# A hybrid encoder layer: when the next block's input is loaded and normed, and when a head's bias rows are requested

## The chip, the cores and the metric

The kernel is one launch on 1 core of one Trainium2 chip. The metric is the device time of the launch in microseconds, as the median of several runs. The engines are TensorE (PE, with its weight loads as PEld), VectorE (DVE), ScalarE (ACT), GpSimd (POOL) and SyncE (SP), which here only issues transfers. Each runs its own instructions in order and waits for the others by semaphores.

## The reference

One layer over 2048 positions of 1024 features in float32. A norm feeds one projection, whose columns go to a state-space part (512 features) and to attention in chunks (8 heads of 64). Both are normed, concatenated, projected and added to x, and a gated feed-forward part of width 2816 follows.

```python
h = rmsnorm(x, norm_mix_g[l])
proj = h @ w_in[l]                      # u_ssm, q, k, v: 512 columns each
y_ssm = s5_mixer(u_ssm, ...)            # diagonal complex scan over the sequence, GLU
y_att = chunked_attention(q, k, v, attn_rel_bias[l])
mixed = concatenate([rmsnorm(y_ssm, ...), rmsnorm(y_att, ...)])
x = x + mixed @ w_out[l]
h2 = rmsnorm(x, norm_ffn_g[l])
x = x + (silu(h2 @ w_gate[l]) * (h2 @ w_up[l])) @ w_down[l]
return rmsnorm(x, norm_final_g)

# chunked_attention: chunks of 64, each sees itself and 8 before it
bias = rel_bias[:, clip(rel, -128, 128) + 128]
scores = einsum('bnqhd,bnkhd->bhnqk', qc, kb) / sqrt(64) + bias
probs = softmax(where(valid, scores, -1e30))
out = einsum('bhnqk,bnkhd->bnqhd', probs, vb)
```

## The kernel before

All of it is one program. After a prologue (norm and the projection for the state-space part) comes the attention part, roughly 135 to 720 us, in which the scan of the state-space part also runs; then the output projection, the gate and up products, and the down product. Only the attention part is touched by the change.

Numbers of full precision are carried through PE as two parts: a high part `hi`, rounded (L741, on ACT), and the rest `lo` (L742, on DVE). A product takes three matmuls: hi with hi, hi with lo, lo with hi. The line of nearly all matmuls is L76, of transposes L79; `split` (L153) does the same for weights, on ACT and DVE.

The attention part runs 128 steps. The sequence is cut in 4 blocks (`sb`) of 512 positions; a block has 4 pairs of heads (`pr`), a pair two heads (`hh`), a head 4 query tiles (`qp`) of 128. So a block is 32 steps and a head 4. Step 0 of block `sb` is step 32 x sb of the part. In each step:

- `scores`: 2 or 4 matmuls `sc` (one PSUM buffer), then on DVE one instruction (L862) that adds the bias rows `nb`, takes the row extreme into `mn` and frees `sc`, and on ACT the exponential (L865).
- `transp`, two steps later: the tile `s` is transposed into `pt` (one PSUM buffer), which ACT copies as `pth` (L880) and DVE as `ptl` (L881).
- `pv_head` after a head's last tile, `pv_scale` after a pair's: matmuls into `pj`, an addition into `ya` on DVE (L905), a scaling, and a store.

The bias rows of a head lie in HBM (`nbs`) and come into one of two buffers, `nba` for even heads and `nbb` for odd ones, by two transfers on SP (L549, L550). `load_nb` asks for those of the next head while a head is in work.

Between the steps lie units of other work, Python generators that are driven forward in a window of steps: `Unit(gen, n, s0, s1, pre)` starts `pre` steps before `s0` and is spread over s0 to s1. `hT_unit` prepares the next block's input: it loads the transposed x in eight pieces of 128 features (L722), multiplies each with the gain and the norm `rsn` in place (L740) and makes `hi` and `lo`. Pieces 0 to 2 (`DB` = 3) go through one unit and tiles `xt` (a ring of 2); pieces 3 to 7 through another, piece 3 in an `xt`, 4 to 7 in pairs in two tiles `raw`, which in block 0 also hold weights that are to be split. `qk_unit` and `v_unit` make q, k and v of a pair of heads for the block from `hi`, `lo` and weights `w` (L707, 1 MB each): k's low part is L788, its store into `ks` L790, the load of the former block's keys L756. `ssm_front` and `ssm_back` are the scan: loads of `U` (L559), `Tm` (L637) and `Vm`, matmuls `pj<-U,Bst`, a long chain on POOL (L603, L604), and `y` (L651).

The order in which the program is written is not the order in which it stands on each engine: PE keeps the written one, and a scheduler orders DVE, ACT, POOL and SP by it and by what it takes each instruction to cost. SP has one queue: a transfer whose source or whose buffer is not ready holds up all behind it.

Of the kernel before, what the change touches and what calls it, by code (L numbers as in the profile page):

```python
# [13 lines left out]
ALU = mybir.AluOpType  # L14
# [4 lines left out]
KT = D // P  # L19
# [6 lines left out]
H, HD = 8, 64  # L26
SB = 512
NSB = SEQ // SB
# [9 lines left out]
SGB = 2  # L38
RA1, RA2 = 2, 12
QS = 4, 5, 6, 7, 0, 1, 2, 3  # L40
HTA = -12, -9
HTS = -8, -6
HTP = 2
PRO = 0, 0, 2, 2, 2, 2, 0, 0, 0
LIGHT = 0.8
SL = 1
# [2 lines left out]
DB, XB = 3, 2  # L49
# [44 lines left out]
def f32(ap):  # L94
    return ap.bitcast(F32)
# [587 lines left out]
def att_phase(k, ident, S, aw, x0, roots):  # L683

    tc, nc, io, pfs = k.tc, k.nc, k.io, k.pfs
    with ExitStack() as cx:
# [28 lines left out]
        def hT_unit(sb, q0=0, q1=KT):  # L715
            hi, lo = hT.setdefault(sb, ([], []))
            ts = slice(sb * SB, (sb + 1) * SB)
            xts = {}

            def load(q, n=1):  # L720
                t = k.t(aw, "raw", [P, 1024], bufs=2) if n > 1 else k.t(aw, "xt", [P, SB], bufs=XB)
                nc.sync.dma_start(t[:].rearrange("p (q t) -> p q t", q=n), io["xt"][q * P : (q + n) * P, ts].rearrange("(q p) t -> p q t", p=P))  # L722
                for m in range(n):
                    xts[q + m] = t[:, m * SB : (m + 1) * SB]

            if q0 == 0:
                load(0)
                load(1)
            else:
                load(q0)  # L730
                for q in range(q0 + 1, q1, 2):
                    load(q, 2)
            for q in range(q0, q1):
                yield
                if q0 == 0 and q + 2 < q1:
                    load(q + 2)
                xt = xts[q]
                for v, n in zip(hT[sb], ("hi", "lo")):
                    v.append(k.t(aw, f"{n}{q}x" if q < DB and sb % 2 else f"{n}{q}", [P, SB], F32R)[:])
                nc.vector.scalar_tensor_tensor(xt, xt, k.gm[:, q : q + 1], S["rsn"][:, ts], op0=ALU.mult, op1=ALU.mult)  # L740
                nc.scalar.copy(hi[q], xt)  # L741
                nc.vector.tensor_tensor(lo[q], xt, f32(hi[q]), op=ALU.subtract)  # L742
            yield

        def qk_unit(sb, pr):
# [47 lines left out]
        QK_N = 1 + 2 * KT  # L793
# [39 lines left out]
        def load_nb(h):  # L833
            return bias_rows(k, S, h, nbt[h % 2])

        def scores(st):
            sb, pr, hh, qp = st
            h = 2 * pr + hh
            if qp == 0:
                hd = st_head[sb, h] = Head()  # L840
                hd.nb = nbs.pop(h) if nbs else load_nb(h)
                hd.s = {}
                hd.p = None
            hd = st_head[sb, h]
            if qp == 2 and (sb, h) < (NSB - 1, H - 1):
                nbs[(h + 1) % H] = load_nb((h + 1) % H)
            q2h, q2l, k2 = qk[sb, pr][hh]
            k0 = max(qp, 4) if sb == 0 else qp
            nk = (qp + 5 - k0) * P
            half = nk // 2 if nk > 512 else nk  # L850
            nch = nk // half
            ps = k.t(psum2, "sc", [P, 2, 512])
            for c in range(nch):
                c0 = k0 * P + c * half + k2.shape[1] - 2 * SB
                cols = slice(c0, c0 + half)
                for n, q2 in ((0, q2h), (1, q2l)):
                    k.ta.matmul(ps[:, c, :half], q2[:, qp * P : (qp + 1) * P], k2[:, cols], start=n == 0, stop=n == 1)
            s = k.t(aa, "s", [P, 640], bufs=3)
            mn = k.t(aa, "mn", [P, 1], bufs=4)
            if (hh, qp) == (0, 0):  # L860
                sums[sb, pr] = k.t(aa, "sm", [P, 2, 4], bufs=3)
            nc.vector.tensor_tensor_reduce(  # L862
                s[:, :nk].rearrange("p (a b) -> p a b", a=nch), ps[:, :nch, :half],
                hd.nb[:, nk - 1 :: -1].rearrange("p (a b) -> p a b", a=nch), 1.0, 3e38, ALU.add, ALU.min, mn[:])
            nc.scalar.activation(s[:, :nk], s[:, :nk], AF.Exp, bias=mn[:], scale=-1.0, accum_out=sums[sb, pr][:, hh, qp : qp + 1])  # L865
            hd.s[qp] = s, k0
# [69 lines left out]
        sp = tc.alloc_tile_pool(name="ssm", reuse_waits="tile", bufs=1)  # L936
        psum = cx.enter_context(tc.tile_pool(name="aps", bufs=1, space=bass.MemoryType.PSUM, reuse_waits="tile"))
        psum2 = cx.enter_context(tc.tile_pool(name="aps2", bufs=1, space=bass.MemoryType.PSUM, reuse_waits="tile"))
        units = []
        for sb in range(NSB):  # L940
            g0 = sb * 32
            C = CUT if sb < NSB - 1 else CUTL
            if sb > 0:
                if DB:
                    units.append(Unit(hT_unit(sb, 0, DB), 2 + DB, g0 + HTA[0], g0 + HTA[1], 2))
                units += [Unit(hT_unit(sb, DB), 2 + KT - DB, g0 + HTS[0], g0 + HTS[1], HTP), Unit(qk_unit(sb, 0), QK_N, g0 + C[0], g0 + C[1], 3, light=LIGHT)]
            units.append(Unit(v_unit(sb, 0), V_N, g0 + C[1], g0 + C[2], 2, light=LIGHT) if sb else Unit(v0, V_N, *V0, done=1))
            for gen, n, c in ((qk_unit(sb, 1), QK_N, 2), (qk_unit(sb, 2), QK_N, 3), (v_unit(sb, 1), V_N, 4), (qk_unit(sb, 3), QK_N, 5)):
                units.append(Unit(gen, n, g0 + C[c], g0 + C[c + 1], 2, light=LIGHT) if sb else Unit(gen, n + 1, C[c], C[c + 1], 4, light=LIGHT, mid=2))
# [5 lines left out]
        for s in range(N + LAG + 2):  # L955
            if s == OPEN:
                aw.release()
                mix = mix_phase(k, S, lambda: k.t(pfs, "pf", [P, 512]))
                units += [Unit(islice(mix, MIX_N), MIX_N, GSTART, N + LAG, GSTART - OPEN)]
            if s == GSTART:  # L960
                sp.release()
            for o in ORDER:
                if o == "s" and s < N:
                    scores(steps[s])
                elif o == "t" and LAG <= s < N + LAG:
                    transp(steps[s - LAG])
                elif o == "p" and LAG + 1 <= s < N + LAG + 1 and steps[s - LAG - 1][3] == 3:
                    pv_head(steps[s - LAG - 1])
                elif o == "p" and s >= LAG + 2 and steps[s - LAG - 2][2:] == (1, 3):
                    pv_scale(steps[s - LAG - 2])  # L970
                elif o == "f":
                    for u in units:
                        u.advance(s)
# [754 lines left out]
```

## Time and profile before

| | |
|---|---|
| median of 3 runs | 2274.19 us (2266.21 to 2277.7) |
| profiled execution, its own time | 2277.4 us |
| span of that execution | 2275.6 us, so 1.8 us lie outside it |
| mean granted clock of PE | 0.978 |
| PE busy | 2169.8 us, 95% of the span |
| DVE / ACT / POOL busy | 68% / 44% / 15% |

The profile is of one execution, which was 3.2 us slower than the median. In a timeline row stand the start, the duration, engine, line, operation, output<-inputs, shape and count; in brackets the idle time of the engine just before it and what ended that. "SPq" rows are transfers being issued, not their landing.

### The profile page before, as it was taken

What the parts mean: (1) busy time and instruction counts of PE and PEld (TensorE: products, weight loads), DVE (VectorE), ACT (ScalarE), POOL (GpSimd) and SP (SyncE); (2) the same over time, 40 slices, a digit from 0 to 9 for tenths busy, and PEclk for the clock granted to TensorE, in tenths of its full rate; (3) what the DMA queues carried; (4) which work ended last, traced back from release to release, by engine and by line L of the source; (5) the groups of instructions that cost most, each with busy time, mean ns of one, the idle gap of its engine ahead of it and who ended that gap; (6) DMA issues with size and microseconds to landing.
All of it is one profiled execution on the core that took longest, in us unless ns stands there. A gap on an engine that the chain in (4) does not pass through costs nothing.

```text
span 2275.6 us, 30307 instructions
## 1 busy us (share of the span) xinstructions
PE 2169.8 (95%) x10632; PEld 1828.5 (80%) x10632; DVE 1542.7 (68%) x2695; ACT 1002.5 (44%) x1656; POOL 350.1 (15%) x827
## 2 busy tenths in 40 slices
PE   8989898999997899999999999999999999999997
PEld 6778787888986688878888887888888777888886
DVE  7757556555556756776767678666666477688776
ACT  6446555455557452343333335333333443353322
POOL 2246666646520000000000000000000010000000
PEclk9999999999998899999999999999999999999999
DMA  8778875766653535854555467655433395465652
GB/s 296 234 250 263 220 195 172 220 197 185 177 166 105 172 118 160 270 179 144 178 183 193 163 213 259 196 175 185 143 93 115 110 389 169 166 226 182 218 179 75
DMA packets 214874, 428.36 MB, mean 188 GB/s; under 512 B 38848, under 2 KB 61424, under 8 KB 207616
## 3 DMA queue, kind: packets, MB, share of 16 engines
q1 hardware_dynamic: 207072, 401.49, 54.6%
q0 software_dynamic: 7648, 24.92, 3.3%
q8 instruction: 84, 1.38, 0.2%
q14 instruction: 70, 0.57, 0.1%
HBM read 286.86 MB, written 129.00 MB: 183 GB/s over the span
## 4 chain that ended last, share of the span: by engine, by line
PE 77%; DMA 5%; DVE 5%; issue 4%; POOL 3%; ACT 2%; SPq 1%; DVEq 0%; ACTq 0%; POOLq 0%
PE X L76 20%; PE ps L76 17%; PE Y L76 10%; PE big L76 9%; PE pf L76 8%; PE W L76 5%; PE pj L76 3%; PE sc L76 2%; DMA acc<-x 2%; PE pt L79 2%; POOL X L595 1%; POOL X L594 1%; DMA lo<-hc 1%; POOL X L604 1%; POOL fx L603 1%
## 5 line engine op out<-in xcount | busy, mean ns | idle before, releaser
L76 PE MATMUL X<-hi,c 128*128 128x512 f32 x1408 | 451.3, 391 | 6.2 <-DVE c L153 5.5
L76 PE MATMUL ps<-hd,hd 128*128 128x512 f32 (+1 forms) x1968 | 429.7, 380 | 3.9 <-DVE hd L153 2.0
L76 PEld LDWEIGHTS ps<-hd,hd 128*128 128x128 f32 x1968 | 357.6, 189 | 74.6 <-DVE hd L153 2.7
L76 PEld LDWEIGHTS X<-hi,c 128*128 128x128 f32 x1408 | 265.4, 189 | 62.7 <-DVE c L153 6.4
L76 PE MATMUL X<-lo,c 128*128 128x512 f32 x704 | 274.9, 390 | 0.0
L153 ACT CAST hd<-hd 128x1536 fp32r<-128x1536 f32 (+1 forms) x106 | 147.3, 1393 | 234.6 <-DMA hd<-hq 148.1
L76 PE MATMUL Y<-hi,c 128*128 128x512 f32 x704 | 224.7, 390 | 2.1 <-DVE u L1407 2.1
L153 DVE TENSOR_TENSOR hd<-hd 128x1536 fp32r<-128x1536 f32 (+1 forms) x106 | 174.0, 1643 | 37.1 <-ACT hd L153 36.5
L153 DVE TENSOR_TENSOR c<-S,c 128x512 fp32r<-128x512 f32 x176 | 120.8, 687 | 98.9 <-ACT c L153 98.7
L1511 POOL DMA_DIRECT2D hd<-hq x7 | 5.3, 762 | 1169.5 <-PE X L76 1158.0
L1403 ACT COPY u<-X 128x512 f32<-128x512 f32 x132 | 77.3, 586 | 200.6 <-PE X L76 200.6
L76 PE MATMUL big<-m,woh 128*128 128x512 f32 x512 | 163.1, 400 | 0.0
L153 ACT CAST c<-S 128x512 fp32r<-128x512 f32 x176 | 109.3, 621 | 119.0 <-PE Y L76 61.8
L1545 DVE TENSOR_TENSOR acc<-acc,ps 128x512 f32<-128x512 f32 x196 | 130.3, 681 | 41.0 <-PE ps L76 40.7
L76 PEld LDWEIGHTS Y<-hi,c 128*128 128x128 f32 x704 | 132.3, 188 | 30.4 <-DVE u L1407 2.9
L76 PEld LDWEIGHTS X<-lo,c 128*128 128x128 f32 x704 | 132.8, 189 | 27.7
L76 PE MATMUL pf<-hi,w 128*128 128x512 f32 x416 | 150.7, 414 | 0.8 <-ACT hi L741 0.8
L153 ACT CAST c<-raw 128x512 fp32r<-128x512 f32 x132 | 82.2, 622 | 151.0 <-PE Y L76 64.3
L881 DVE TENSOR_TENSOR ptl<-pt,pth 128x640 fp32r<-128x640 f32 (+3 forms) x152 | 98.2, 646 | 66.6 <-ACT pth L880 64.8
L76 PE MATMUL Y<-lo,c 128*128 128x512 f32 x352 | 137.0, 389 | 0.0
L865 ACT ACTIVATE s<-s,mn 128x640 f32<-128x640 f32 (+4 forms) x128 | 97.9, 765 | 74.1 <-DVE mn L862 67.1
L880 ACT CAST pth<-pt 128x640 fp32r<-128x640 f32 (+3 forms) x152 | 83.6, 550 | 82.6 <-PE pt L79 77.6
(448 smaller groups left out, 4280.6 us busy)
## 6 DMA issues: line engine op xcount, KB each, us to landing
w<-wss SPq DMA_DIRECT2D x36, 1024.0 KB, 6.6
hq<-g SPq DMA_DIRECT2D x140, 256.0 KB, 2.1
hd<-hq SPq DMA_DIRECT2D x35, 768.0 KB, 4.5
hd<-wc SPq DMA_DIRECT2D x35, 768.0 KB, 5.9
raw<-in_w_gate SPq DMA_DIRECT2D x44, 512.0 KB, 3.7
raw<-in_w_up SPq DMA_DIRECT2D x44, 512.0 KB, 4.2
wc<-px SPq DMA_DIRECT2D x66, 256.0 KB, 2.9
wss<-w SPq DMA_DIRECT2D x12, 1024.0 KB, 5.8
```

The lines of the kernel that those rows point to most:

```text
L76: return self.tc.keep_in_program_order(self.tc.nc.tensor.matmul(*a, **b))
L79: return self.tc.keep_in_program_order(self.tc.nc.tensor.transpose(*a, **b))
L153: return nc.scalar.copy(hi, raw), nc.vector.tensor_tensor(lo, raw, f32(hi), op=ALU.subtract)
L594: eng.tensor_tensor(dst, dst, t[:, :, :, :n], op=ALU.add)
L595: eng.tensor_tensor(dst, dst, t2[:, :, :, :n], op=ALU.add)
L603: eng.tensor_tensor(t, end[:, e].unsqueeze(3).to_broadcast([P, GP, n, 7]), pw, op=ALU.mult)
L604: eng.tensor_tensor(dst[:, c], dst[:, c], t, op=ALU.subtract if e == 1 and c == 0 else ALU.add)
L865: nc.scalar.activation(s[:, :nk], s[:, :nk], AF.Exp, bias=mn[:], scale=-1.0, accum_out=sums[sb, pr][:, hh, qp : qp + 1])
L880: nc.scalar.copy(pth[:, a:b, qp, :], pt[:, a:b, :])
L881: nc.vector.tensor_tensor(ptl[:, a:b, qp, :], pt[:, a:b, :], f32(pth[:, a:b, qp, :]), op=ALU.subtract)
L1403: nc.scalar.copy(u[:], ps[:])
L1545: V.tensor_tensor(a, a, ps[:], op=ALU.add)
```

## The change

Three things are changed; all matmuls, their number and their order on PE stay as they are.

The window of the unit of pieces 0 to 2 goes from steps -12 to -9 (before the block's first step) to -16 to -13. The unit of pieces 3 to 7 is cut in two: the loads and the norms, one norm for each advance, in steps -13 to -8 with one step ahead, and the hi and lo parts in -8 to -6. The bias rows of the next head are requested in a head's second step (`qp == 1`) instead of its third.

```diff
-HTA = -12, -9
+HTA = -16, -13
 HTS = -8, -6
-HTP = 2
+HTN = -13, -8
...
+            def norm(q):
+                nc.vector.scalar_tensor_tensor(xts[q], xts[q], k.gm[:, q : q + 1], S["rsn"][:, ts], op0=ALU.mult, op1=ALU.mult)
+
             if q0 == 0:
                 load(0)
                 load(1)
...
                 for q in range(q0 + 1, q1, 2):
                     load(q, 2)
+                for q in range(q0, q1):
+                    yield
+                    norm(q)
             for q in range(q0, q1):
                 yield
-                if q0 == 0 and q + 2 < q1:
-                    load(q + 2)
-                xt = xts[q]
+                if q0 == 0:
+                    if q + 2 < q1:
+                        load(q + 2)
+                    norm(q)
...
-                nc.vector.scalar_tensor_tensor(xt, xt, k.gm[:, q : q + 1], S["rsn"][:, ts], op0=ALU.mult, op1=ALU.mult)
-                nc.scalar.copy(hi[q], xt)
-                nc.vector.tensor_tensor(lo[q], xt, f32(hi[q]), op=ALU.subtract)
+                nc.scalar.copy(hi[q], xts[q])
+                nc.vector.tensor_tensor(lo[q], xts[q], f32(hi[q]), op=ALU.subtract)
...
-            if qp == 2 and (sb, h) < (NSB - 1, H - 1):
+            if qp == 1 and (sb, h) < (NSB - 1, H - 1):
                 nbs[(h + 1) % H] = load_nb((h + 1) % H)
...
+        hts = {sb: hT_unit(sb, DB) for sb in range(1, NSB)}
...
-                units += [Unit(hT_unit(sb, DB), 2 + KT - DB, g0 + HTS[0], g0 + HTS[1], HTP), ...]
+                units += [Unit(islice(hts[sb], 1 + KT - DB), 1 + KT - DB, g0 + HTN[0], g0 + HTN[1], 1), Unit(hts[sb], 1 + KT - DB, g0 + HTS[0], g0 + HTS[1]), ...]
```

Behind line 721 the changed file's lines are 5 or 6 higher: the norm is L727, hi L747, lo L748, k's low part L794, L862 is L868 and L881 is L887.

On the engines this gives, at three places, the following order. On DVE at steps 17 to 19, where block 1's input is prepared (`w<-raw` is a weight's split, `lo0x` to `lo2x` are low parts, `nba` marks the bias addition of a step), before:

```order
366 L153 TENSOR_TENSOR w_2436<-raw_2360,w_2436 128x1024
367 L862 ISA s_2402,mn_2403<-sc_2399,nba_106 128x256
369 L881 TENSOR_TENSOR ptl_2293<-pt_2406,pth_2292 128x128
370 L820 SCALAR_TENSOR_TENSOR v_483_2249<-pf_2380,no_1236,v_483_2249 128x4x64
371 L881 TENSOR_TENSOR ptl_2293<-pt_2406,pth_2292 128x3x128
372 L862 ISA s_2447,mn_2448<-sc_2444,nba_106 128x384
374 L740 SCALAR_TENSOR_TENSOR xt_2487<-xt_2487,g_mix_86,rsn_92 128x512
375 L153 TENSOR_TENSOR w_2439<-raw_2362,w_2439 128x1024
376 L742 TENSOR_TENSOR lo0x_2559<-xt_2487,hi0x_2558 128x512
377 L905 TENSOR_TENSOR ya_2279<-pj_2455,yt_2464 64x512
```

and after, from the reduction of step 17 on:

```order
369 L868 ISA s_2420,mn_2421<-sc_2417,nba_106 128x256
371 L887 TENSOR_TENSOR ptl_2293<-pt_2424,pth_2292 128x128
372 L153 TENSOR_TENSOR w_2454<-raw_2364,w_2454 128x1024
373 L748 TENSOR_TENSOR lo1x_2412<-xt_2323,hi1x_2411 128x512
374 L887 TENSOR_TENSOR ptl_2293<-pt_2424,pth_2292 128x3x128
375 L826 SCALAR_TENSOR_TENSOR v_483_2251<-pf_2384,no_1236,v_483_2251 128x4x64
376 L153 TENSOR_TENSOR w_2457<-raw_2366,w_2457 128x1024
377 L727 SCALAR_TENSOR_TENSOR xt_2403<-xt_2403,g_mix_86,rsn_92 128x512
378 L868 ISA s_2468,mn_2469<-sc_2465,nba_106 128x384
380 L911 TENSOR_TENSOR ya_2279<-pj_2476,yt_2485 64x512
381 L748 TENSOR_TENSOR lo2x_2462<-xt_2403,hi2x_2461 128x512
382 L887 TENSOR_TENSOR ptl_2489<-pt_2490,pth_2488 128x128
```

Both splits, a low part and a norm now stand ahead of the reduction of step 18 (row 378; 372 before), and a further low part ahead of the ptl of row 382.

On SP at steps 23 and 24 (`U` is what the scan's next batch reads, `ks` the stores of k, `k<-ks` the load of keys), before:

```order
130 L651 DMA y_65<-U_1705 16x4x256 x7
131 L722 DMA raw_2675<-in_xt 128x2x512
132 L559 DMA Bst_2686<-bsts_70 128x512
133 L559 DMA U_2677<-u_64 16x16x64 x8
134 L790 DMA ks_68<-k_536_2514 128x512
135 L790 DMA ks_68<-k_539_2517 128x512
136 L756 DMA k_594_2752<-ks_68 128x512
```

and after:

```order
131 L651 DMA y_65<-U_1705 16x4x256 x8
132 L796 DMA ks_68<-k_546_2537 128x512
133 L796 DMA ks_68<-k_549_2540 128x512
134 L762 DMA k_596_2758<-ks_68 128x512
135 L559 DMA U_2681<-u_64 16x16x64 x8
```

The loads of U moved from ahead of the two `ks` stores and the key load to behind them; the input load and Bst are issued earlier.

On DVE at steps 55 and 56, where block 2's input is prepared, before:

```order
565 L862 ISA s_4511,mn_4512<-sc_4506,nbb_1549 128x640
567 L881 TENSOR_TENSOR ptl_4464<-pt_4515,pth_4463 128x5x128
568 L891 RECIPROCAL rs_4685<-sm_4050 128x8
569 L788 TENSOR_TENSOR k_920_4282<-pf_4403,k_920_4282 64x512
570 L788 TENSOR_TENSOR k_923_4285<-pf_4403,k_923_4285 64x512
571 L862 ISA s_4561,mn_4562<-sc_4556,nba_106 128x640
573 L881 TENSOR_TENSOR ptl_4464<-pt_4566,pth_4463 128x5x128
574 L740 SCALAR_TENSOR_TENSOR xt_4482<-xt_4482,g_mix_86,rsn_92 128x512
575 L740 SCALAR_TENSOR_TENSOR raw_4484<-raw_4484,g_mix_86,rsn_92 128x512 x2
576 L742 TENSOR_TENSOR lo_993_4575<-xt_4482,hi_992_4574 128x512
```

and after:

```order
570 L748 TENSOR_TENSOR lo_993_4580<-xt_4253,hi_992_4579 128x512
571 L868 ISA s_4515,mn_4516<-sc_4510,nbb_1549 128x640
573 L748 TENSOR_TENSOR lo_995_4584<-raw_4255,hi_994_4583 128x512
574 L887 TENSOR_TENSOR ptl_4473<-pt_4519,pth_4472 128x5x128
575 L897 RECIPROCAL rs_4685<-sm_4054 128x8
576 L748 TENSOR_TENSOR lo_997_4588<-raw_4255,hi_996_4587 128x512
577 L748 TENSOR_TENSOR lo_999_4592<-raw_4257,hi_998_4591 128x512
578 L794 TENSOR_TENSOR k_930_4305<-pf_4418,k_930_4305 64x512
579 L748 TENSOR_TENSOR lo_1017_4664<-raw_4257,hi_1016_4663 128x512
580 L868 ISA s_4566,mn_4567<-sc_4561,nba_106 128x640
```

The norms are gone from here, and four low parts stand ahead of k's low part (L794; L788 before), where none stood.

In SP's order the two requests for the bias rows of step 72 move from behind the loads of U of that batch to either side of the `ya` store that stood 10 rows ahead of them; those for step 60 keep their place behind a key load, seven loads into `rsn` and one of Bst. In block 3 the loads of pieces 3 to 7, though their unit starts sooner, stand later in SP's order than before, and their norms later on DVE; the requests for step 80 stand behind the eight `y` stores instead of ahead of them.

More of the change, by code (lines that the diff above doesn't have):

```diff
@@ L945, in att_phase @@
                     units.append(Unit(hT_unit(sb, 0, DB), 2 + DB, g0 + HTA[0], g0 + HTA[1], 2))
-                units += [Unit(hT_unit(sb, DB), 2 + KT - DB, g0 + HTS[0], g0 + HTS[1], HTP), Unit(qk_unit(sb, 0), QK_N, g0 + C[0], g0 + C[1], 3, light=LIGHT)]
+                units += [Unit(islice(hts[sb], 1 + KT - DB), 1 + KT - DB, g0 + HTN[0], g0 + HTN[1], 1), Unit(hts[sb], 1 + KT - DB, g0 + HTS[0], g0 + HTS[1]), Unit(qk_unit(sb, 0), QK_N, g0 + C[0], g0 + C[1], 3, light=LIGHT)]
             units.append(Unit(v_unit(sb, 0), V_N, g0 + C[1], g0 + C[2], 2, light=LIGHT) if sb else Unit(v0, V_N, *V0, done=1))
```

## The prediction

> **What bounds the kernel now.** I read the page first, then the busy time by window over the attention part, then the timelines of TensorE, VectorE and the SP queue around each stretch in which TensorE stood still.
>
> ```profile
> span 2275.6 us, 30307 instructions
> PE 2169.8 (95%) x10632; PEld 1828.5 (80%) x10632; DVE 1542.7 (68%) x2695; ACT 1002.5 (44%) x1656; POOL 350.1 (15%) x827
> ```
>
> TensorE (PE) is busy for 95% of the span, so a change that leaves its instructions alone can only close holes in it. The change touches only the attention part; the windows there have start:end, length, PE's busy time with its instructions, the granted clock, the DMA share and GB/s.
>
> ```profile
> 205.00:245.00 40.00, 31.29 (x146) 0.83 0.90 239
> ...
> 372.00:412.00 40.00, 30.34 (x154) 0.91 0.69 203
> ...
> 460.00:500.00 40.00, 35.58 (x210) 0.96 0.73 211
> ...
> sum 540.00, PE 502.74; mean PE 62.84
> ```
>
> Of the 540 us from 150 to 690, PE is busy for 502.74: 37.3 us of holes, 1.6% of the span, is all that could be won. Half lies in two windows: 8.7 us in 205 to 245 and 9.7 us in 372 to 412, and there the granted clock is low too (0.83 and 0.91). The holes that the change can reach are these, with the idle time before the row and its releaser in brackets:
>
> ```profile
> 210.41 0.69 PE L79 MATMUL pt<-ident,s 128*128 128x128 f32 x2 [2.31 <-DVE ptl L881]
> ...
> 240.77 3.75 PE L76 MATMUL pj<-U,Bst 128*128 128x256 f32 x8 [4.20 <-DMA ks<-k]
> ...
> 377.30 0.42 PE L76 MATMUL sc<-k,q2h 128*128 128x320 f32 x1 [1.31 <-DVE k L788]
> ...
> 382.43 0.50 PE L76 MATMUL pf<-hi,w 128*128 128x512 f32 x1 [0.80 <-ACT hi L741]
> ...
> 386.52 0.80 PE L76 MATMUL pf<-lo,w 128*128 128x512 f32 x1 [3.58 <-DVE lo L742]
> ...
> 406.79 0.38 PE L76 MATMUL sc<-k,q2h 128*128 128x320 f32 x1 [3.75 <-DVE mn L862]
> ...
> 466.11 0.43 PE L76 MATMUL sc<-k,q2h 128*128 128x320 f32 x1 [2.64 <-DVE mn L862]
> ...
> 492.82 0.41 PE L76 MATMUL sc<-k,q2h 128*128 128x320 f32 x1 [1.59 <-DVE mn L862]
> ```
>
> Some holes cost more than their own length. The same run of matmuls, in an undisturbed step and behind a hole:
>
> ```profile
> 460.08 0.31 PE L76 MATMUL sc<-k,q2h 128*128 128x320 f32 x1
> ...
> 462.38 0.63 PE L76 MATMUL pf<-hi,w 128*128 128x512 f32 x2
> ...
> 470.07 0.63 PE L76 MATMUL pf<-hi,w 128*128 128x512 f32 x2
> ```
>
> From the scores at 460.08 to the pf at 462.38 takes 2.30 us; the same stretch from 466.11 (in the list of holes) to 470.07 takes 3.96, so the hole of 2.64 us is followed by a slow stretch that costs 1.66 more. The first pf behind the 3.58 us takes 0.80, the one in front of that hole (382.43) 0.50, so it has such a tail too. The scores behind 3.75 us at 406.79 take 0.38, about as without a hole, so not every hole has one. I count 1.66 with the two holes that show it, and half of that, 0.8, with a new one of over 2.5 us.
>
> [...]
>
> **The change part by part.** PE's order is the same before and after; so are the counts of every kind of instruction. The terms are therefore holes that open, close or move.
>
> *Block 1's inputs, prepared in block 0 (a loss).* VectorE's (DVE's) order moves three norms (L740, now L727) and three low parts (L742, now L748) ahead of where they stood, into the stretch in which it also splits two weights (L153). The last four rows are of later places; three of them show what the same operations take there.
>
> ```profile
> 201.27 1.23 DVE L153 TENSOR_TENSOR w<-raw,w 128x1024 fp32r<-128x1024 f32 x1 [0.52 <-ACT w L153]
> ...
> 202.75 0.29 DVE L881 TENSOR_TENSOR ptl<-pt,pth 128x128 fp32r<-128x128 f32 x1
> 203.16 0.48 DVE L820 SCALAR_TENSOR_TENSOR v<-pf,no,v 128x256 fp32r<-128x256 f32 x1
> 204.01 0.56 DVE L881 TENSOR_TENSOR ptl<-pt,pth 128x384 fp32r<-128x384 f32 x1 [0.37 <-ACT pth L880]
> 204.49 0.55 DVE L862 CUSTOM_DVE_ANT_0 s<-sc,nba 128x384 f32<-128x384 f32 x1
> 204.96 0.75 DVE L740 SCALAR_TENSOR_TENSOR xt<-xt,g_mix,rsn 128x512 f32<-128x512 f32 x1
> 205.63 2.24 DVE L153 TENSOR_TENSOR w<-raw,w 128x1024 fp32r<-128x1024 f32 x1
> 207.79 1.52 DVE L742 TENSOR_TENSOR lo0x<-xt,hi0x 128x512 fp32r<-128x512 f32 x1
> 209.34 0.68 DVE L905 TENSOR_TENSOR ya<-pj,yt 64x512 f32<-64x512 f32 x1
> ...
> 231.91 1.40 DVE L788 TENSOR_TENSOR k<-yt,k 64x512 fp32r<-64x512 f32 x2
> ...
> 380.10 1.63 DVE L740 SCALAR_TENSOR_TENSOR xt<-xt,g_mix,rsn 128x512 f32<-128x512 f32 x1
> ...
> 384.94 1.52 DVE L742 TENSOR_TENSOR lo<-xt,hi 128x512 fp32r<-128x512 f32 x1
> ...
> 529.58 0.69 DVE L742 TENSOR_TENSOR lo<-xt,hi 128x512 fp32r<-128x512 f32 x1 [0.44 <-ACT hi L741]
> ```
>
> Before, the reduction of step 18 (L862 at 204.49) comes before both the norm and the second split. After, between the ptl that ends at 203.04 and that reduction stand: split, lo1x, ptl 0.56, v 0.48, split, norm. At the short prices (split 1.23, then 2.24; norm 0.75; 0.69 for the low part, as at 529.58) that is 5.95 us: the reduction starts at 209.0 instead of 204.5. The next scores need its PSUM buffer; behind it come ya 0.68, lo2x 0.69 and ptl 0.29. They end at about 211.3, and the matmul that waits for this ptl stood at 210.41, so its hole grows by 0.9 us at the short prices. At the long ones (split 2.24 twice, low parts 1.52, norms 1.63, as at 380.10) it grows by 4.4 us. POOL works through this stretch, and one split and the low part above show the long price, one split and the norm the short one; I take 1.9.
>
> The SP queue, in order, decides the next hole, which waits for the loads of U (L559):
>
> ```profile
> 226.87 4.19 SPq L651 DMA_DIRECT2D y<-U  x7
> 231.10 0.43 SPq L722 DMA_DIRECT2D raw<-in_xt  x1
> ...
> 233.14 4.58 SPq L559 DMA_DIRECT2D U<-u  x8
> 237.90 0.81 SPq L790 DMA_DIRECT2D ks<-k  x2
> ```
>
> Before, U is issued at 233.14 and only then the two ks stores. After, the input load at 231.10 is gone from here, but both ks and a key load stand ahead of U. The ks wait for the two L788 (231.91 above), which end at 233.3 before and come one low part later (0.69): 234.0, then 0.4 for a ks and 0.4 for the key load; U starts at 234.8, 1.7 us later. That is +1.7; nothing if the ks slip by, 2.5 if the low part costs 1.52. The delay of L788 also widens the wait for the scores just ahead, but inside the same 1.7. Sum of the block: +3.6 us (0.9 to 6.9).
>
> *Block 2's low and high parts (a gain).* Before, the whole preparation of the last five inputs stands between two matmuls, with the norm and the low part at 380.10 and 384.94 (above) in it.
>
> After, the norms run some steps sooner and the first low part too, so 0.80 + 3.58 + 1.66 of tail = 6.0 us go. What is late next is the wait at 377.30: two more low parts now stand ahead of the first L788. At 0.69 each they push it by 0.65 us (DVE had some room there); at 1.52 each, as beside POOL's long operations, by 2.25. With 2.25 the hole is 3.56 us and may get a tail of its own. I take that case, since both rows at 380.10 and 384.94 were long beside POOL: 6.0 - 2.25 - 0.8 = 3.0 us gained (5.4 at the short price, 2.1 with a full tail).
>
> *Bias rows one step sooner.* Of the two waits on bias rows (406.79 and 466.11), one goes and one stays. SP's requests around them, and the next one:
>
> ```profile
> 400.77 0.45 SPq L549 DMA_DIRECT2D nbb<-nbs  x1
> ...
> 442.59 0.32 SPq L915 DMA_DIRECT2D ya_s<-ya  x1
> ...
> 461.12 0.47 SPq L549 DMA_DIRECT2D nba<-nbs  x1
> ...
> 482.96 0.73 SPq L549 DMA_DIRECT2D nba<-nbs  x1
> ```
>
> The rows for step 72 are requested at 461.12 and 0.5 us later, behind four moves of q, loads of Tm, Vm and U. After, they stand next to the ya store of 442.59, 18 us earlier, and the scores at 463.4 no longer wait: 2.64 + 1.66 = 4.3 us gained. Nothing else was due there: PE's next work runs on without a hole in the step before. The rows for step 60 (400.77) stand in the same place of SP's order after, behind a key load that waits for PE, seven loads into rsn and one of Bst: the 3.75 us at 406.79 stay.
>
> *Block 3's inputs (a gain).* DVE stood for 2.28 us at a norm whose input had not landed, with L788 and the next reduction queued behind it:
>
> ```profile
> 490.44 0.75 DVE L740 SCALAR_TENSOR_TENSOR raw<-raw,g_mix,rsn 128x512 f32<-128x512 f32 x1 [2.28 <-DMA raw<-in_xt]
> ```
>
> After, these loads and norms come later in both queues, so the 1.59 us at 492.82 go. What is late next: the rows for step 80, requested at 482.96 before, now stand behind the eight y stores of this stretch, some 12 us later, and the inputs stand behind two loads of weights. I estimate about a microsecond of room for each, put nothing down for them, and take 1.5 and 1.2 us as the upper ends.
>
> **Sum.** +3.6 - 3.0 - 4.3 - 1.6 = -5.3 us. The profiled execution took 2277.4 us, 3.2 above the median of 2274.19: 2272.1 in its terms, 2268.9 in those of the median. With every bound at its good end it is 0.9 - 5.4 - 4.3 - 1.6 = -10.4 (2263.8), with every bound at its bad end 6.9 - 2.1 - 4.3 - 1.6 + 2.7 = +1.6 (2275.8), before the spread of the runs (2266.21 to 2277.7).
>
> **The rivals.**
>
> *The pile-up on DVE in block 0 decides (slower).* Place: the reduction of step 18. If POOL's work overlaps all of its new neighbours, each of the long prices applies: 4.4 there, a hole of over 6 us in all and so with a tail of its own that the 2.31 us had only in part (up to 1.66), and U is then 2.5 late: 8.6. If at 377 the new wait also takes the place of the old holes wholly (0 in place of -3.0) and the waits of 463 and 492 go as said (-5.9), the sum is +2.7, 2276.9. With the other terms as forecast, it is slower from the point at which block 0 costs more than 8.9 us (3.0 + 4.3 + 1.6). For it: splits and low parts at double price stand in the rows above. Against: the norm at 204.96 was at the short price in the same stretch. To be slower by over 0.5% a new late transfer in block 3 of some 8 us would have to come on top. Chance 0.17.
>
> *All waits go and nothing takes their place (faster).* DVE is idle for short stretches between 198 and 202, so the first norms fit there, and U is not late: block 0 costs nothing; at 377 the short price holds (-5.4); 463 and 492 give 5.9; sum -11.3, 2262.9. For it: DVE is busy for only 68% of the span. Against: rows such as 207.79. Chance 0.23.
>
> *The bias rows still wait.* If the sooner request is held by the keys ahead of it, step 72 stays as it is: -5.3 + 4.3 = -1.0, 2273.2. Against it: what stands ahead of it then is issued at 442 at the latest. Chance 0.05.
>
> **How the numbers follow.** The forecast has the remaining 0.55. About 0.5%, 11.4 us, is what a measurement of this kernel tells from no change. Faster by more than that is the half of the second rival and a little of the forecast that lie beyond it, with what I may have missed: 0.24. Slower by more is the part of the first rival with late transfers, and again what I may have missed in an order of this length: 0.16. The rest, 0.60, is within. The range reaches from the second rival to the first, each moved out by 8 us, the distance of the lowest run from the median (2262.9 - 8, 2276.9 + 8): 2255 to 2285.
>
> **What would show it.** Right: no hole over 1 us before the scores of step 72, nor at what was 382 to 386; a hole of 3 to 4 us around what was 207 to 211, in two parts, with the reduction of step 18 late; U issued behind two ks; the hole on the nbb rows of step 60 still near 3.7; a wait on L788 (now L794) of 2 to 3.5 us in block 2. Wrong: the first of these still there, or a hole on nba rows of step 80 or on norms waiting for inputs in block 3. What would turn the sign is more than 8.9 us of holes in 200 to 245 beyond those of before.

## The result and the profile after

The changed kernel takes 2265.56 us (median of 18 runs, 2263.25 to 2269.63), the kernel before 2274.98 beside it (18 runs, 2266.21 to 2282.92). The ratio is 0.996, with a 95% interval of 0.9951 to 0.9969: 9.4 us faster, or 7 to 11. The forecast was 2268.9; its sum gave 5.3 us of the 9.4.

The page of the changed kernel, its span and the busy time of each engine:

```profile
span 2261.8 us, 30301 instructions
...
PE 2164.9 (96%) x10632; PEld 1826.8 (81%) x10632; DVE 1540.2 (68%) x2695; ACT 1003.6 (44%) x1656; POOL 351.9 (16%) x827
```

Its own time was 2263.53. The span is 13.8 us shorter than in the profile of before, more than the medians differ: 2.3 us of it lie in the prologue, where both kernels run the same instructions.

The three windows of the attention part that the prediction showed (start:end, length, PE's busy time and instructions, granted clock, DMA share, GB/s), now of the changed kernel:

```profile
205.00:245.00 40.00, 31.11 (x143) 0.88 0.91 259
...
372.00:412.00 40.00, 33.29 (x187) 0.96 0.76 237
...
460.00:500.00 40.00, 39.47 (x271) 1.00 0.69 218
```

The first window is as it was (8.9 us of holes, 8.7 before); in the second the holes went from 9.7 to 6.7 and in the third from 4.4 to 0.5, each at a higher clock (0.83 before and 0.88 now, 0.91 and 0.96, 0.96 and 1.00; the work in them lies up to 12 us sooner than before; of the places shown, only the scores of step 72 have left their window by that, which are at 455.97 now). PE's timeline at the places of the holes, in the changed kernel (the idle time before the row and its releaser in brackets):

```profile
205.89 0.44 PE L76 MATMUL pj<-ptl,v 128*128 128x384 f32 x1 [1.43 <-DVE ptl L887]
...
210.19 0.44 PE L79 MATMUL pt<-ident,s 128*128 128x128 f32 x2 [0.47 <-DVE ptl L887]
...
240.45 3.78 PE L76 MATMUL pj<-U,Bst 128*128 128x256 f32 x8 [4.54 <-DMA U<-u]
...
375.75 0.41 PE L76 MATMUL sc<-k,q2h 128*128 128x320 f32 x1 [1.88 <-DVE k L794]
...
398.32 0.38 PE L76 MATMUL sc<-k,q2h 128*128 128x320 f32 x1 [3.95 <-DVE mn L868]
...
455.97 0.31 PE L76 MATMUL sc<-k,q2h 128*128 128x320 f32 x1
...
491.42 0.38 PE L76 MATMUL sc<-k,q2h 128*128 128x320 f32 x1 [0.33 <-DVE mn L868]
...
505.66 0.55 PE L79 MATMUL pt<-ident,s 128*128 128x128 f32 x3 [0.67 <-DVE ptl L887]
```

The norm's and the low part's holes of block 2 (0.80 and 3.58) are gone, the wait on k's low part rose only from 1.31 to 1.88, the scores of step 72 (455.97) wait for nothing, and the 3.75 us of step 60 are still there as 3.95. The scores of step 78, which waited 1.59 us at 492.82 before, stand at 479.27 without a hole; the row at 491.42 is of step 81.

Of the signs that the prediction named, the holes of step 72 and of 382 to 386 went, U stands behind two ks, the hole of step 60 stayed, and no hole of step 80 or of a norm waiting for its input came. Two sizes missed: the hole around 207 to 211 came in three parts of 2.15 us in all (3 to 4 said), and the wait on L794 was 1.88 (2 to 3.5 said).

**Shifts by stretch.** A profile starts a few us early or late for reasons outside the change, so the stretches are compared inside each run: the start of a step's reduction (L862, now L868) counted from step 0's, and the difference of that to the first profile of before. For step 58, the four rows are these, of before and of the changed kernel on DVE:

```profile
136.96 0.29 DVE L862 CUSTOM_DVE_ANT_0 s<-sc,nba 128x128 f32<-128x128 f32 x1 [2.19 <-PE sc L76]
...
391.43 0.82 DVE L862 CUSTOM_DVE_ANT_0 s<-sc,nba 128x640 f32<-128x640 f32 x1 [0.96 <-PE sc L76]
```

```profile
134.64 0.29 DVE L868 CUSTOM_DVE_ANT_0 s<-sc,nba 128x128 f32<-128x128 f32 x1 [2.13 <-PE sc L76]
...
382.76 0.82 DVE L868 CUSTOM_DVE_ANT_0 s<-sc,nba 128x640 f32<-128x640 f32 x1 [1.12 <-PE sc L76]
```

(382.76 - 134.64) - (391.43 - 136.96) = -6.35 us: so much sooner stands step 58. The same for all profiles, between the steps at a column's head; the change of block 1's input falls into the first two columns, of block 2's into the third, the wait for `nbb` of step 60 into the fourth, for `nba` of step 72 into the fifth, block 3's input into the last. The sooner request for the bias rows also changes orders in the first two columns and the last one, as shown below:

| profile | 0-28 | 28-55 | 55-58 | 58-63 | 63-74 | 74-87 |
|---|---|---|---|---|---|---|
| before, again | -1.38 | +0.01 | -0.28 | +2.53 | -1.17 | +0.42 |
| after | +2.23 | -2.02 | -6.56 | +1.37 | -4.51 | -0.31 |
| after_again | +3.41 | +0.46 | -6.45 | +1.56 | -4.51 | -0.27 |
| after_5 | +4.41 | -2.07 | -6.55 | -0.06 | -4.46 | -0.02 |
| e1_bias | +0.60 | -0.20 | -0.49 | +2.29 | -4.45 | -1.22 |
| e2_input | +1.63 | -0.34 | -5.92 | +1.72 | -0.45 | +0.59 |
| e5_b23 | +3.48 | -1.25 | -6.53 | +1.78 | -4.49 | -0.29 |
| e6_qp0 | +2.06 | -0.56 | -4.92 | -3.11 | -4.46 | -1.86 |
| e7_b23_qp0 | +0.64 | +1.53 | -4.86 | -2.80 | -4.45 | -0.68 |
| e9_b2 | -1.95 | -0.24 | -5.92 | +1.28 | +1.77 | -1.86 |
| e10_b1 | +0.40 | -0.69 | -0.71 | +2.91 | +0.44 | -0.08 |
| e11_b3 | -2.14 | +0.02 | -0.45 | +2.93 | -1.24 | -0.27 |
| e12_b2_qp0 | +0.37 | -0.23 | -6.53 | -2.62 | -4.45 | -1.86 |

Each row is one execution; two of the same kernel differ by up to 2.5 us in a column. The means that are used below are over all profiles with a part of the change against all without it.

### The profile page after: what moved, and what is told of

It is laid out like the page before. It is cut to its first block, busy times and chain, and to the rows that moved or that the text cites. A ratio compares the mean times of both kernels' runs of the same rounds, so it can differ in the third digit from the quotient of the medians.

```text
span 2261.8 us, 30301 instructions
## 1 busy us (share of the span) xinstructions
PE 2164.9 (96%) x10632; PEld 1826.8 (81%) x10632; DVE 1540.2 (68%) x2695; ACT 1003.6 (44%) x1656; POOL 351.9 (16%) x827
## 4 chain that ended last, share of the span: by engine, by line
PE 82%; issue 3%; POOL 3%; DVE 3%; DMA 2%; ACT 2%; SPq 0%; DVEq 0%; ACTq 0%; POOLq 0%
PE X L76 21%; PE ps L76 19%; PE Y L76 11%; PE big L76 9%; PE pf L76 9%; PE W L76 5%; PE pj L76 4%; PE sc L76 2%; PE pt L79 2%; POOL st L592 1%; POOL X L595 1%; POOL X L594 1%; POOL X L604 1%; POOL fx L603 0%; POOL st L593 0%
## 5 line engine op out<-in xcount | busy, mean ns | idle before, releaser
L887 DVE TENSOR_TENSOR ptl<-pt,pth 128x640 fp32r<-128x640 f32 (+3 forms) x152 | 98.2, 646 | 60.1 <-ACT pth L886 58.7
L871 ACT ACTIVATE s<-s,mn 128x640 f32<-128x640 f32 (+4 forms) x128 | 97.9, 765 | 67.7 <-DVE mn L868 60.7
```

What stands on the lines that cost most here:

```text
L887: nc.vector.tensor_tensor(ptl[:, a:b, qp, :], pt[:, a:b, :], f32(pth[:, a:b, qp, :]), op=ALU.subtract)
```

## The experiments

Ratios are to the kernel before, run in the same comparison, with their 95% intervals. An edit lets the scheduler order other work anew too, so a run with one edit alone does not leave the rest of the kernel as it was.

**The bias rows alone**, in the kernel before:

```diff
-            if qp == 2 and (sb, h) < (NSB - 1, H - 1):
+            if qp == 1 and (sb, h) < (NSB - 1, H - 1):
```

> Before, with only the bias rows requested in a head's second step. If the request itself closes the wait of step 72 (hole 2.64 us and 1.66 us of slow matmuls behind it) and does nothing else: 4.3 us faster than before, the hole on L862 near 463 gone, all other holes as before. If the whole gain of the change comes from the input's preparation: no difference.

Measured: 2272.93 us against 2276.8, ratio 0.9982 (0.9968 to 0.9995): 4.1 us, 3.9 by the medians. The table has 4.45 in the stretch of step 72, and no gain clear of the scatter before it. The request alone brings what was put down for it, with no help from the input. But it does something else too. In block 0, SP now has both `ks` stores ahead of U, as in the changed kernel:

```profile
232.80 1.04 SPq L790 DMA_DIRECT2D ks<-k  x2
...
234.02 3.79 SPq L559 DMA_DIRECT2D U<-u  x8
```

And in block 3, DVE comes to the first norm 395.9 us after step 0, where before did it at 342.0, and the hole of 1.59 us is gone (-1.22 in the last column):

```profile
531.93 0.73 DVE L740 SCALAR_TENSOR_TENSOR xt<-xt,g_mix,rsn 128x512 f32<-128x512 f32 x1
```

**The input alone**: the changed kernel with the request back in the third step.

```diff
-            if qp == 1 and (sb, h) < (NSB - 1, H - 1):
+            if qp == 2 and (sb, h) < (NSB - 1, H - 1):
```

> The changed kernel, with the bias rows requested in the third step as before: only the input's preparation is new. If the two parts are independent: 9.4 - 4.3 = about 5 us faster than before, with a hole near 455 to 460 of about 2.6 us on the bias rows of step 72 again. If the input's preparation is all of it: 9.4 us faster.

Measured: 2270.55, ratio 0.998 (0.9963 to 0.9997): 4.6 us, 6.2 by the medians. 0.18% and 0.20% make 0.38%, against 0.40% for both together: within their intervals, the two parts add. Step 72 has its wait back on PE:

```profile
462.69 0.38 PE L76 MATMUL sc<-k,q2h 128*128 128x320 f32 x1 [2.23 <-DVE mn L868]
```

**The input by blocks.** In e5, block 1's input is prepared as before and everything else as in the changed kernel. The generator yields its norms apart only in the blocks listed, and the windows go by a second list with the same blocks:

```diff
+HTA0 = -12, -9
+SPLIT = (2, 3)
+HTAN = (2, 3)
...
-                for q in range(q0, q1):
-                    yield
-                    norm(q)
+                if sb in SPLIT:
+                    for q in range(q0, q1):
+                        yield
+                        norm(q)
...
+                if q0 == 0 or sb not in SPLIT:
                     norm(q)
...
+                    ha = HTA if sb in HTAN else HTA0
...
+                if sb in SPLIT:
...
+                else:
+                    units.append(Unit(hts[sb], 2 + KT - DB, g0 + HTS[0], g0 + HTS[1], 2))
```

> The changed kernel, but block 1's input is prepared as before (old windows, loads, norms and parts in one unit); blocks 2 and 3 as changed. By the prediction's term for block 0 this is 3.6 us faster than the changed kernel; by the two traces (the matmul at 166.28 came 2.3 us sooner after, the one at 292.06 0.9 sooner) 1.4 us faster; if block 0 only traded one hole for another, the same.

Measured: 2265.41, ratio 0.9954 (0.9938 to 0.997), not to be told from the changed kernel's 0.996. By the medians block 1's part costs little or nothing. The profile taken of e5 was the slowest of its runs (2271.96) and lost 3.48 us in the first column. It has block 1's old preparation, but not before's order: with the sooner request both `ks` stores stand ahead of U here too, which starts 99.7 us after step 0 (96.2 in before).

Then each block alone, with the request as before (`qp == 2`): both lists `(1,)`, `(2,)` and `(3,)`.

> Before, with only block 1's input prepared the new way (loads, norms and parts in block 0). By the prediction's term: 3.6 us slower than before. By the traces of before and after: later by 2.2 us at step 28, of which the wait for the scan at 289 gives back what it gives back; 0 to 2 us slower at the end. If the matmuls behind the shorter holes at 210 and 292 run at full clock: the same as before.

> Before, with only block 2's input prepared the new way, bias rows as before. By the prediction's term 3.0 us faster. By the traces (the two holes at 382 and 386 with what follows: step 58 came 6.4 us sooner after), 6 us faster up to step 58; if the next hole (bias rows of step 60) is then followed by slow matmuls, as after and not as before, 4.5 us faster at the end.

> Before, with only block 3's input prepared the new way. By the prediction's term 1.6 us faster than before (the hole of 1.59 us goes and nothing takes its place). By the two profiles of the changed kernel, where the same stretch came only 0.3 to 0.4 us sooner, the norms at steps 83 and 84 take back most of it: 0 to 0.5 us, not to be told from before.

Measured, each over 12 runs: block 1 alone 2275.78, ratio 1.0004 (0.9987 to 1.0021); block 2 alone 2270.21, 0.998 (0.9964 to 0.9995); block 3 alone 2274.48, 0.9999 (0.9984 to 1.0013). Block 2 carries the whole gain of the input's part; by the ratios block 1 costs 0.9 us with an interval of some 4 to each side, block 3 brings 0.2 us with one of some 3, so neither is told from nothing.

**The request one step sooner still**, in the head's first step, in the changed kernel:

```diff
-            if qp == 1 and (sb, h) < (NSB - 1, H - 1):
+            if qp == 0 and (sb, h) < (NSB - 1, H - 1):
```

> The changed kernel, with the bias rows requested in a head's first step. The request for step 60 then stands ahead of the key load that waits for TensorE. If that wait is what held it, the hole of 3.95 us at 394 goes with the slow matmuls behind it (about 1.6 us): 4 to 5.5 us faster than the changed kernel. If the rows would be late anyway, or if what they now delay on the queue costs as much: the same or slower.

Measured: 2262.97, ratio 0.9948 (0.9931 to 0.9965). That is some 2.6 us below the changed kernel in another comparison, less than the 4 to 5.5 expected. This is about the hole of step 60, which the change left. The SP queue of the changed kernel around the requests for step 60 (`nbb`) and step 72 (`nba`):

```profile
387.81 0.34 SPq L762 DMA_DIRECT2D k<-ks  x1
388.19 3.44 SPq L559 DMA_DIRECT2D rsn<-u  x7
...
392.25 0.47 SPq L549 DMA_DIRECT2D nbb<-nbs  x1
...
434.69 0.45 SPq L549 DMA_DIRECT2D nba<-nbs  x1
```

The request for `nbb` (392.25) stands behind the key load and eight further loads; the one for `nba` has moved from 461.12 to 434.69. In e6 the `nbb` request passes the key load on SP:

```profile
378.79 0.47 SPq L549 DMA_DIRECT2D nbb<-nbs  x1
...
392.08 0.34 SPq L762 DMA_DIRECT2D k<-ks  x1
```

and on PE the scores of step 60 follow without a hole; the next wait is one of 1.23 us on the scan's tile, at 404.70:

```profile
394.96 0.31 PE L76 MATMUL sc<-k,q2h 128*128 128x320 f32 x1
...
404.70 0.50 PE L76 MATMUL pj<-pth,v 128*128 128x512 f32 x1 [1.23 <-ACT X L578]
```

The table has -3.11 in that stretch where the changed kernel has -0.06 to +1.56.

**The sooner request with fewer blocks**: blocks 2 and 3 (`SPLIT = (2, 3)`), and block 2 alone (`SPLIT = (2,)`), both with `qp == 0`.

> Blocks 2 and 3 prepared the new way, block 1 as before, bias rows requested in the first step. By the same count 13 us below before: equal to the kernel with block 2 alone if block 3 brings nothing, 1 to 2 us faster than that if the sooner request also removes what block 3's norms ran into.

> Only block 2's input prepared the new way, blocks 1 and 3 as before, bias rows requested in a head's first step. If block 1's new preparation costs 1 to 2 us and block 3's brings nothing: 1 to 2 us faster than the same with all three blocks (2262.97 us in its own comparison, 11.8 below before), so 13 to 14 below before. If the parts lean on each other: no faster than that.

Measured: 2263.19, ratio 0.9949 (0.9931 to 0.9967), and 2263.4, 0.9946 (0.9925 to 0.9967), over 6 runs each. Neither differs from e6, and the 13 to 14 us expected did not come. All three lie some 12 us below before, 2.6 to 3.6 below the medians of the changed kernel; the intervals of the ratios overlap, so that they beat the changed kernel is likely by medians and by the stretch of step 60, not shown by the ratios alone. e12's profile is 15.3 us ahead at step 87 and loses 5 of it by step 100, in part in new waits on PE for weights (1.44 us at 554.75 and 1.38 at 573.51).

**Both kernels again, unchanged**, for what one profile is worth, and the changed kernel over 11 runs beside e7, e11 and e12:

> The kernel before, unchanged, for a second profile. If the slow matmuls behind a hole follow from the program, the same holes are followed by slow matmuls as in the first profile: those at 210, 292, 386 and 466, and not the one at 406. If they follow from the phase of something that runs freely, others are.

> The changed kernel, unchanged, for a second profile. If slow matmuls follow from the program: behind the hole at 398, and not behind those at 210 and 291. If from the phase of something free-running: others. Holes themselves within 0.5 us of those of the first profile.

> The changed kernel once more, as the measure for the three beside it on the same chip: 9 us faster than before.

Measured: 2272.98 and 2269.26 in single runs; after_5 2266.79 against 2275.23, ratio 0.996 (0.9947 to 0.9974), the first result once more. What stands behind the holes was not the same in the second profiles (see the tails below). Nor were all holes within 0.5 us: in the changed kernel the one at U was 4.54 us in the first profile, 5.72 in the second and 7.11 in after_5.

## Why the prediction was right, and its sizes wrong

The direction, the waits at step 72 and in block 2, and the range held; the sum was too small, for the most part because of one term. The change of 9.4 us lies between the forecast's 5.3 and the second rival's 11.3, nearer to the rival, whose short price in block 2 is the one that came. By the table:

| term | predicted | measured, profiles with a part of the change against those without | the changed kernel's three profiles against before's two |
|---|---|---|---|
| block 0 | +3.6 | +1.6 for block 1's input (columns 1 and 2: mean +1.49 with, -0.09 without) | +2.8 |
| block 2 | -3.0 | -5.6 (-6.03 with, -0.39 without) | -6.4 |
| hole of step 60 | 0 | left as it was | -0.3 |
| step 72 | -4.3 | -4.4 (-4.47 with, -0.11 without) | -3.9 |
| block 3 | -1.6 | -0.2 for block 3's input (ratio of e11) | -0.4 |
| sum | -5.3 | | -8.2; by the medians of all runs -9.4 |

The errors partly cancel: block 2 brought 2.6 to 3.4 us more than was put down, block 3 about 1.2 less. That the sum came within some 4 us is luck to that extent.

**Block 2: the price of the low parts.** This is the step that failed. The prediction took 1.52 us for each of two low parts ahead of L794, "since both rows at 380.10 and 384.94 were long beside POOL", and so 2.25 us of new wait and 0.8 of tail. DVE in the changed kernel:

```profile
371.74 0.69 DVE L748 TENSOR_TENSOR lo<-raw,hi 128x512 fp32r<-128x512 f32 x1
...
373.59 1.39 DVE L748 TENSOR_TENSOR lo<-raw,hi 128x512 fp32r<-128x512 f32 x2 [0.31 <-ACT hi L747]
375.01 0.68 DVE L794 TENSOR_TENSOR k<-pf,k 64x512 fp32r<-64x512 f32 x1
375.73 0.69 DVE L748 TENSOR_TENSOR lo<-raw,hi 128x512 fp32r<-128x512 f32 x1
```

Each took 0.69; the hole grew by 0.57, near the 0.65 of the short price, which gave -5.4. In the other profiles with block 2's new preparation the wait on k's low part is as short, 1.88 to 1.98 us (after_5, e2, e5, e6, e7, e9, e12). The tail of 0.8 did not come here either: the 3 us behind the wait ran at a clock of 1.00. It came in e6 and e7 (0.74 and 0.67), whose third column (-4.9) is 1 us and more short of that of the seven others, which had 1.00. The price was paid elsewhere. POOL in the changed kernel:

```profile
371.78 0.72 POOL L592 TENSOR_TENSOR st<-X,a 128x4 f32<-128x4 f32 x1
...
373.73 0.70 POOL L604 TENSOR_TENSOR X<-X,fx 128x42 f32<-128x42 f32 x1
374.52 0.59 POOL L603 TENSOR_TENSOR fx<-X,a 128x42 f32<-128x42 f32 x1
...
375.90 0.67 POOL L604 TENSOR_TENSOR X<-X,fx 128x42 f32<-128x42 f32 x1
376.66 1.06 POOL L603 TENSOR_TENSOR fx<-X,a 128x434 f32<-128x434 f32 x1
```

and in the kernel before, where DVE has no low part here:

```profile
372.32 0.21 POOL L592 TENSOR_TENSOR st<-X,a 128x4 f32<-128x4 f32 x1
...
373.75 0.31 POOL L604 TENSOR_TENSOR X<-X,fx 128x42 f32<-128x42 f32 x1
374.14 0.27 POOL L603 TENSOR_TENSOR fx<-X,a 128x42 f32<-128x42 f32 x1
...
375.59 1.06 POOL L603 TENSOR_TENSOR fx<-X,a 128x434 f32<-128x434 f32 x1
```

The POOL operations above that start within a low part take 0.59 to 0.72 instead of 0.21 to 0.31, and end 0.07 to 0.15 us behind the low part's row: four low parts that keep their 0.69, four long small operations. POOL's long operations, beside which DVE's were long at 380.10, begin at 376.66, behind the low parts. Measured from step 0 that is 3.4 us later than before (242.0 against 238.6); how much of it the low parts themselves caused was not tried. POOL beside the two low parts at the long price, in the kernel before (DVE's rows of 207.79 and 384.94, 1.52 each, stand in the prediction):

```profile
206.86 1.91 POOL L604 TENSOR_TENSOR X<-X,fx 128x434 f32<-128x434 f32 x1
...
384.54 1.38 POOL L604 TENSOR_TENSOR X<-X,fx 128x434 f32<-128x434 f32 x1
```

and beside one in the changed kernel, DVE's row first:

```profile
199.43 0.73 DVE L748 TENSOR_TENSOR lo0x<-xt,hi0x 128x512 fp32r<-128x512 f32 x1
...
199.70 1.39 POOL L603 TENSOR_TENSOR fx<-X,a 128x434 f32<-128x434 f32 x1
```

The low part took 1.52 where POOL's operation had begun 0.93 and 0.40 us before it, 0.73 where it began 0.27 behind the low part, and then POOL's took 1.39 (1.05 to 1.07 at 380.13, 381.79 and 383.40 before). The norm of 380.10 (1.63) does not tell: its row begins 0.03 us before POOL's of 380.13. The two rows of before were reason to ask which of the two starts first in the new place, and how long POOL's operations there are, instead of carrying over the price of a place 6 us on; by them alone the short price was likely, not sure.

**Block 0: the mechanism came, but not from block 1's input alone.** DVE in the changed kernel:

```profile
202.10 1.80 DVE L153 TENSOR_TENSOR w<-raw,w 128x1024 fp32r<-128x1024 f32 x1
203.82 1.54 DVE L748 TENSOR_TENSOR lo1x<-xt,hi1x 128x512 fp32r<-128x512 f32 x1
...
206.15 1.21 DVE L153 TENSOR_TENSOR w<-raw,w 128x1024 fp32r<-128x1024 f32 x1
207.28 0.74 DVE L727 SCALAR_TENSOR_TENSOR xt<-xt,g_mix,rsn 128x512 f32<-128x512 f32 x1
207.94 0.55 DVE L868 CUSTOM_DVE_ANT_0 s<-sc,nba 128x384 f32<-128x384 f32 x1
...
209.24 0.69 DVE L748 TENSOR_TENSOR lo2x<-xt,hi2x 128x512 fp32r<-128x512 f32 x1
```

One split and one low part at nearly the long price, the rest short, and the reduction of step 18 late (207.94; measured from step 0, 5.8 us later than 204.49 of before). The matmul at 210.19 stands 2.1 us later from step 0 than its like at 210.41 (1.9 were put down). But the hole of 2.31 has become holes of 1.43, 0.25 and 0.47, and what follows is quicker: the same 107 matmuls from there to U's take 22.98 us of PE instead of 23.96, at a clock of 0.91 instead of 0.84. That was a tail behind before's 2.31 us, which the forecast's sum left out, and which that execution had by chance (see the tails below). For U, SP in the changed kernel:

```profile
224.79 6.19 SPq L651 DMA_DIRECT2D y<-U  x8
231.41 1.06 SPq L796 DMA_DIRECT2D ks<-k  x2
232.56 0.40 SPq L762 DMA_DIRECT2D k<-ks  x1
233.13 3.75 SPq L559 DMA_DIRECT2D U<-u  x8
```

The order is as forecast, two ks and a key load ahead of U, and U starts 2.3 us later from step 0 (1.7 put down). The hole at U grew only from 4.20 to 4.54 in this profile, since PE was later too; in the other two of the changed kernel it was 5.72 and 7.11. Behind it another part is given back in this profile at a wait for the scan, 2.20 us where before had 3.05.

The prediction put all of this down to block 1's input. The runs show that the sooner request alone also moves U behind the ks (e1, above). The start of U's loads on SP, counted from step 0, and in brackets the mean shift of columns 1 and 2 together:

| | block 1's input as before | prepared the new way |
|---|---|---|
| request in the third step | 94.9 to 96.2 (before twice, e9, e11) [-1.4] | 97.7 and 98.4 (e10, e2) [+0.5] |
| request sooner | 97.9 to 99.7 (e1, e5, e7, e12) [+1.2] | 98.5 to 100.7 (changed kernel three times, e6) [+2.0] |

So either edit delays U by some 3 us, and both together by some 4. In the shifts, which scatter by up to 3.7 us within a group, block 1's input costs 0.7 to 1.9 and the request 1.5 to 2.7. By the times of whole runs e10 can't tell block 1's part from nothing.

**Step 72** came out as predicted in eight profiles of eight that have a sooner request (-4.45 to -4.51). These are counted from before's first profile, whose hole there had a tail (a clock of 0.53 in the 3 us behind 466.11). Against other profiles with the late request it is 3.2 (e11, with a clock of 1.00 behind the hole) to 6.2 (e9, with a hole of 4.69), so that the mean of 4.4 agrees so well with 4.3 is in part chance.

**Step 60** stays for the reason given: in e6, e7 and e12, where the request stands ahead of the key load, the hole is gone. In the changed kernel SP stands 2.6 us at that key load, waiting for scores on PE, and the eight loads behind it take the rest up to the request. In e6 the request has also passed loads of Tm and Vm that are issued before the key load, so what the wait for PE alone costs is not separated.

**Block 3** brought little of its 1.6, and not for the reason put down. The prediction had the loads and norms come later by the new preparation. With that and the late request (e11, e2) they come no later: the first norm is at 341.6 and 340.1 us from step 0 (342.0 before), four norms of the pairs of pieces (3.72 us in e11) stand ahead of the reduction of step 76 where two did (1.88), and a hole of 1.59 and 1.27 us comes one step sooner. PE in e11:

```profile
486.62 0.42 PE L79 MATMUL sc<-k,q2h 128*128 128x320 f32 x1 [1.59 <-DVE mn L873]
```

It is the sooner request that moves them (e1, above). In the changed kernel, with both, the hole is gone and the norms, in the first profile at 356 to 373 us from step 0, stand elsewhere in the way. DVE in the changed kernel:

```profile
502.16 2.71 DVE L727 SCALAR_TENSOR_TENSOR raw<-raw,g_mix,rsn 128x512 f32<-128x512 f32 x2
504.79 0.81 DVE L887 TENSOR_TENSOR ptl<-pt,pth 128x640 fp32r<-128x640 f32 x1
505.52 0.97 DVE L727 SCALAR_TENSOR_TENSOR raw<-raw,g_mix,rsn 128x512 f32<-128x512 f32 x1
```

Two norms (2.71) ahead of a `ptl` that PE waits for (0.67 at 505.66). The prediction called "what is late next" a microsecond of room and put nothing down. In the last column the request with the old preparation has -1.22 and -1.86 (e1, e12), with the new one -0.02 to -1.86 (mean of six -0.57): the new preparation of block 3 seems to take back some of what the request gives, which executions that scatter so do not settle.

**The tails.** The prediction had slow matmuls behind 2.64 us and none behind 3.75, both from one profile. The clock in the 3 us behind the hole of step 60 (columns as for the windows), in before's first profile and then in the same kernel's second:

```profile
406.79:409.79 3.00, 3.00 (x17) 1.00 0.98 362
...
210.41:213.41 3.00, 3.00 (x8) 0.50 0.97 214
```

```profile
404.32:407.32 3.00, 3.00 (x11) 0.50 0.99 357
208.94:211.94 3.00, 3.00 (x14) 1.00 0.95 220
```

The same two holes (3.75 us in one profile and 3.70 in the other, and 2.31 in both), and the clocks exchanged: the missing tail was a chance of that execution. Over all 14 profiles, 160 to 560 us, the 3 us behind a hole ran at a clock of 1.00 in 14 of 17 cases behind 1.5 to 2.1 us, in 10 of 36 behind 2.1 to 3.4 and in 2 of 44 behind more. Holes of 2.1 to 3.4 us so had a lower clock behind them in 26 of 36 cases, in 12 of them 0.55 or less over the 3 us; what sets the clock in a given execution no run shows. The 1.66 behind 2.64 us was so a likely tail, not a sure one.

## What to carry to other kernels

An operation's price next to another engine is not a constant to carry from one place to the next: look at what that engine runs at the new place, and which of the two starts first (here a low part on DVE took 1.52 us where a long operation of POOL had begun 0.40 us before it, at 384.94 before, and 0.69 where a small one began 0.04 us behind it, at 371.74 in the changed kernel). A request that stands behind a load waiting for PE can cost a stall however short it is itself (0.47 us on SP here): moving it past that load and others around it took the hole of step 60 away (3.95 us in the changed kernel's first profile and 3.68 in after_5, none in e6, e7 and e12). One edit to the order of a program lets its scheduler move other work: check in the trace what else moved before putting a place down to an edit, here the loads of U and the norms of block 3, which the request moves and not only the input's preparation. Before calling a behaviour of one profile a property, take the profile again: here terms of 2 us and less changed from one execution to the next.

## What the runs showed of the hardware

The granted clock in the 3 us behind the same hole of the same program was 1.00 in one execution and 0.50 in another (406.79 in before's first profile, 404.32 in its second). A POOL operation on 128x4 took 0.72 us beside a low part on DVE (371.78 in the changed kernel) and 0.21 with nothing under way on DVE (372.32 before). The y stores ahead of U held SP for 6.19 and 7.30 us in two profiles of the changed kernel, the first and after_5 (eight, 0.77 and 0.91 each), and for 4.19 before (seven, 0.60 each); what holds them up was not tried.
